# mLSTM heads: squares and denominators folded to 64 partitions each and summed by one product with a two-column selector; memory tokens' squares added over their two parts before they are summed

## The chip, the cores and the metric

One core of one Trainium2 chip. The metric is the device time of one execution in microseconds (us). Matrix products run on TensorE (PE in the profile; its weight loads are PEld), elementwise work on VectorE (DVE), ScalarE (ACT) and GpSimd (POOL); SyncE (SP) issues the DMAs.

## The reference, cut to what matters

One decoder layer, 1024 tokens of width 1024, float32. The part that is changed are the four mLSTM heads (width 128 each) and the norm of 256 memory tokens.

```python
def rmsnorm(x, g):
    xf = x.astype(jnp.float32)
    y = xf * lax.rsqrt(jnp.mean(xf * xf, axis=-1, keepdims=True) + EPS)
    return (y * g.astype(jnp.float32)).astype(x.dtype)
...
        # mlstm_chunkwise, per head, t over tokens
        den = scores.sum(-1) + inter * jnp.einsum('bhd,bhtd->bht', n, qc)
        h = num / jnp.maximum(jnp.abs(den), jnp.exp(-m_t))[..., None]
...
        mh = mlstm_chunkwise(mq, mk, mv, ig, lf)
        mh = mh * lax.rsqrt(jnp.mean(mh * mh, axis=-1, keepdims=True) + EPS)
...
        x = x + cross_attention(rmsnorm(x, ln_x[l]), rmsnorm(mem, ln_mem[l]), w_xq[l], w_xkv[l], w_xo[l])
```

Of each mLSTM head and token two sums over a column are needed: the denominator `den` (over the 128 source rows of the weighted scores) and the sum of the squares of `num` (over the head's 128 columns).

## The kernel before

All large products are split in two parts and made by three products each, `mm3` (L190-194: low by high, high by low, high by high). Every product into float32 has a stationary operand of 128x128 that PEld loads, and up to 512 columns that move past it. The parts themselves come from `split` (L135-142: ACT copies the high part, DVE subtracts it for the low part).

The kernel is written as a sequence of stages, and a scheduler of the framework interleaves them: it sets the order of the instructions of each engine from dependencies and from the program's order, outside stretches that are pinned with `in_order()`. Tiles come from rings of buffers: `w2("c")` is one of two tiles of 128x512 named r_c, `w2("b")` one of two r_b, and the PSUM banks are three sc, two tp, one mm, one m2 (m in the profile) and one ov. An instruction that wants a tile waits until the tile that had the buffer before is read for the last time.

Where the work around the change lies in time (read from the rows of its lines): memory tokens are prepared at about 40 to 100 us (`mem_prepare`, L289-308), and the four heads at about 100 to 395 us. Between and beside the heads' own products PE makes the projections of the next head (`ml_project`), and beside the last head the values of the forgetting attention: `token_major(..., fv_sink)` makes 256-column products into banks tp, mm and m2, and `fv_sink` (L661-664) evacuates each with an ACT copy (L141) and a DVE subtraction (L142) into a tile that rotates over r_b, r_p and r_c. The first scores of the forgetting attention (L754-755) and their masks (L734) come in there too.

In `ml_head` each head is made in two halves of 512 tokens. In a half, for each block of 128 source rows, the scores come from `mm3` into sc, are weighted on DVE (L599), split (L601), and added up over the blocks by GpSimd into `acc` (L603, 128x512, tile r_b); the value products (L605) add up into bank ov. After the last of them the numerator is brought to SBUF (first half: ACT copies it, L613, and squares it, L614; second half: DVE adds the carried part, L609, and ACT squares that, L610), and `sum_cols` (L230-232) makes the column sums on PE: four products with the 128x128 slices of `acc` as weights and one moving column of ones, and four more with the slices of the squares `sq` (tile r_c). ACT takes the absolute denominators (L618) and DVE copies the sums of squares (L619). After the second half follow a chain of small DVE and GpSimd operations that gives the factor of each token, its way through DRAM to a row (`to_row`, L254-261), and the scaling of the numerators (L640-645).

`mem_prepare` adds up the squares of pairs of 128-row slices, so its `acc` of 128x512 has two parts of 256 tokens; `rsqrt_sums` (L243-250) sums both parts with four products of one moving column (two tokens' blocks by two parts).

Of the kernel before, what the change touches and what calls it, by code (L numbers as in the profile page):

```python
# [11 lines left out]
AF = mybir.ActivationFunctionType  # L12
ALU = mybir.AluOpType
# [4 lines left out]
P = 128  # L18
# [4 lines left out]
NM = 256  # L23
# [21 lines left out]
def hybrid_layer(ctx: ExitStack, tc: tile.TileContext, a: dict, out: bass.AP):  # L45
    nc = tc.nc
    v, s, g = nc.vector, nc.scalar, nc.gpsimd
# [11 lines left out]
    def sb(tag, shape, bufs, dt=F32):  # L59
        return pool.tile(shape, dt, tag=tag, name=name(tag), bufs=bufs)  # L60
# [18 lines left out]
    def w2(tag, n=512, dt=F32, p=P):  # L79
        return sb("r_" + tag, [P, 512], BUFS[tag], dt)[:p, :n]  # L80

    def col(tag, n=1, bufs=3):
        return sb("c_" + tag, [P, 8], bufs)[:, :n]
# [3 lines left out]
    def ps_tile(tag):  # L87
        return psum.tile([P, 512], F32, tag=tag, name=name(tag), bufs=PBUFS[tag])

    def sc():  # L90
        return ps_tile("sc")
# [4 lines left out]
    def ov_():  # L96
        return ps_tile("ov")
# [10 lines left out]
    def const(n, shape, dt=F32):  # L108
        return pool.tile(shape, dt, tag=n, name=n, bufs=1)
# [7 lines left out]
    for _ in range(11):  # L117
        nc.tensor.matmul(spun, blank[:, :P], blank, start=True, stop=True)

    ones = const("ones", [P, 1])  # L120
    g.memset(ones, 1.0)
    ident = const("ident", [P, P])
    g.memset(ident, 1.0)
    g.affine_select(out=ident, in_=ident, pattern=[[-1, P]], compare_op=ALU.is_equal, fill=0.0, base=0, channel_multiplier=1)
# [10 lines left out]
    def split(hi, lo, src, scale=None):  # L135

        if scale is None:
            s.activation(hi, src, AF.Copy)  # L138
            return v.tensor_tensor(out=lo, in0=src, in1=hi.bitcast(F32), op=ALU.subtract)  # L139
        else:  # L140
            s.activation(hi, src, AF.Copy, scale=scale)  # L141
            return v.scalar_tensor_tensor(out=lo, in0=src, scalar=scale, in1=hi.bitcast(F32), op0=ALU.mult, op1=ALU.subtract)  # L142
# [53 lines left out]
    def both(pair, f):  # L196
        return f(pair[0]), f(pair[1])
# [32 lines left out]
    def sum_cols(ps, src, n):  # L230
        for t in range(n):
            nc.tensor.matmul(ps[:, t : t + 1], src[:, t * P : (t + 1) * P], ones, start=True, stop=True)

    def square_sum(acc, x, first, by=s, add=v):
        sq = acc if first else w2("c")[:, : x.shape[-1]]
        if by is s:
            s.activation(sq, x, AF.Square)
        else:
            by.tensor_tensor(out=sq, in0=x, in1=x, op=ALU.mult)
        if not first:  # L240
            add.tensor_tensor(out=acc, in0=sq, in1=acc, op=ALU.add)

    def rsqrt_sums(acc, r, nt, parts=1, bank=None, over=None, how=rsqrt_cols):  # L243

        ps = (bank or ov_)()
        for t in range(nt):
            for e in range(parts):
                at = (e * nt + t) * P
                nc.tensor.matmul(ps[:, t : t + 1], acc[:, at : at + P], ones, start=e == 0, stop=e == parts - 1)
        return how(r, ps[:, :nt], 1.0 / D, nt, over)  # L250
# [36 lines left out]
    rcol_m = const("rcol_m", [P, 2])  # L287

    def mem_prepare():  # L289
        acc = w2("b")  # L290
        for i in range(KT // 2):
            if i == 2:
                yield
            raw = w2("f")
            load(raw.rearrange("p (k c) -> p k c", k=2), a["mem"][:, 2 * i : 2 * i + 2])
            hi = w2("p", dt=F32R)
            with tc.issue_after(begun):
                square_sum(acc, raw, i == 0)
                for e in range(2):
                    c = slice(e * NM, e * NM + NM)  # L300
                    gain = vec[:, VEC["ln_mem"] + 2 * i + e :][:, 0:1]
                    split(hi[:, c], raw[:, c].bitcast(F32R), raw[:, c], gain)
            for p_, t in enumerate((hi.bitcast(F32), raw)):
                load(hmd[:, p_, 2 * i : 2 * i + 2], t.rearrange("p (k c) -> p k c", k=2))
        yield
        rsqrt_sums(acc, rcol_m, 2, 2)
        to_row(row_m, rcol_m, 2, rowd[1:2, :NM])
        yield

# [7 lines left out]
    def mv_of(hd, t):  # L317

        return mv[hd // 2][:, t, hd % 2 * 256 : hd % 2 * 256 + 256]
# [15 lines left out]
    for k in range(KT):  # L335
        if k % 2 == 0:
            c = slice(k % 4 * 256, k % 4 * 256 + 512)
# [44 lines left out]
    z, e, q, lf = (small[:, i:j].rearrange("p (t c) -> p t c", c=c) for i, j, c in ((0, 128, GC), (128, 224, GW), (224, 320, GW), (320, 416, GW)))  # L382
# [58 lines left out]
    ps = ov_()  # L441
# [136 lines left out]
    def ml_head(hd, q, k, og, num1, den1):  # L578
        fac = col("fac", 8)
        nums = []  # L580
        dens = col("dens", 8)
        sqs = col("sqs", 8)
        for hf in range(2):
            nmb = w2("a")
            load(nmb, rows[hd : hd + 1, hf * TH : hf * TH + TH].broadcast_to([P, TH]))
            num = ov_()
            acc = den1 if hf else w2("b")
            last = 4 * hf + 3
            for j in range(4 * hf, last + 1):
                d0 = j - 4 * hf  # L590
                c0 = min(d0 * P, 256)
                sp = sc()
                ks = both(k, lambda z: z[:, j * P : (j + 1) * P])
                mm3(sp[:, c0:], ks, both(q, lambda z: z[:, hf * TH + c0 : hf * TH + TH]), True, True)
                wt = acc if j == 0 else w2("c")
                s.activation(wt[:, c0:], nmb[:, c0:], AF.Exp, bias=gcol[:, j, hd : hd + 1])
                n_ = d0 * P + P - c0
                g.affine_select(out=wt[:, c0 : c0 + n_], in_=wt[:, c0 : c0 + n_], pattern=[[1, n_]], compare_op=ALU.is_ge, fill=0.0, base=c0 - d0 * P, channel_multiplier=-1)
                v.scalar_tensor_tensor(out=wt[:, c0:], in0=sp[:, c0:], scalar=float(P) ** -0.5, in1=wt[:, c0:], op0=ALU.mult, op1=ALU.mult)  # L599
                wh, wl = w2("d", dt=F32R), w2("e", dt=F32R)  # L600
                split(wh[:, c0:], wl[:, c0:], wt[:, c0:])  # L601
                if j:
                    g.tensor_tensor(out=acc[:, c0:], in0=wt[:, c0:], in1=acc[:, c0:], op=ALU.add)  # L603
                vj = mv_of(hd, j)
                mm3(num[:, c0:], (vj[:, :P], vj[:, P:]), (wh[:, c0:], wl[:, c0:]), d0 == 0, j == last)  # L605
            sq = w2("c")
            if hf:
                nsb = num1
                v.tensor_tensor(out=nsb, in0=num, in1=nsb, op=ALU.add)  # L609
                s.activation(sq, nsb, AF.Square)  # L610
            else:
                nsb = w2("f")
                s.activation(nsb, num, AF.Copy)  # L613
                s.activation(sq, num, AF.Square)  # L614
            ps = sc()
            sum_cols(ps[:, 0:4], acc, 4)
            sum_cols(ps[:, 4:8], sq, 4)
            s.activation(dens[:, 4 * hf : 4 * hf + 4], ps[:, 0:4], AF.Abs)  # L618
            v.tensor_copy(sqs[:, 4 * hf : 4 * hf + 4], ps[:, 4:8])  # L619
            nums.append(nsb)  # L620
        v.tensor_tensor(out=dens, in0=dens, in1=emc[:, :, hd], op=ALU.max)
        rd = col("rd", 8)
        v.reciprocal(rd, dens)
        v.tensor_tensor(out=sqs, in0=sqs, in1=rd, op=ALU.mult)
        v.tensor_tensor(out=sqs, in0=sqs, in1=rd, op=ALU.mult)
        rsqrt_cols(fac, sqs, 1.0 / P, 8)
        v.tensor_tensor(out=fac, in0=fac, in1=rd, op=ALU.mult)
        yield
        end = hd == MLH - 1
        fbs = [w2("a"), w2("d")] if end else [None, None]  # L630
        at = facd[hd : hd + 1]
        for hf in range(2):
            fb = fbs[hf] or w2("a")
            if hf == 0:
                to_row(fb, fac, 8, at, sc)
            if hf != end:
                load(fbs[1] or fb, at[:, TH:].broadcast_to([P, TH]))
            yield
            y = nums[hf]
            v.scalar_tensor_tensor(out=y, in0=y, scalar=vec[:, VEC["ml_norm"] + hd : VEC["ml_norm"] + hd + 1], in1=fb, op0=ALU.mult, op1=ALU.mult)  # L640
            v.scalar_tensor_tensor(out=y, in0=og[:, hf * TH : hf * TH + TH], scalar=1.0, in1=y, op0=ALU.add, op1=ALU.mult)
            yh, yl = w2("e" if end and hf else "y", dt=F32R), y.bitcast(F32R)
            split(yh, yl, y, 0.5)
            load(mix[hf, 0, :, hd], yh.bitcast(F32))
            load(mix[hf, 1, :, hd], yl.bitcast(F32))
# [59 lines left out]
    for _ in range(2):  # L705
        t = act().rearrange("p a b -> p (a b)").rearrange("p (i c) -> p i c", i=4)
# [403 lines left out]
    for step in fill:  # L1110
        n, e = divmod(halves[0], 2)
# [479 lines left out]
    for at, (b, m) in enumerate(steps):  # L1591
# [14 lines left out]
        x = x2[m // 2][:, m % 2]  # L1606
# [3 lines left out]
        for i, of, y, op in ((1, 1, x22, ALU.add), (5, 5, x22, ALU.add), (7, 7, x22, ALU.add), (6, 6, x22, ALU.add), (2, 1, x11, ALU.add), (4, 5, x21, ALU.subtract), (3, 7, x12, ALU.subtract)):  # L1610
            if of == i:
                held[of] = bank()
            ps = held[of]
# [9 lines left out]
    for i in range(2):  # L1623
        t = act()
# [132 lines left out]
```

## Time and profile before

| what | value |
|---|---|
| median of 3 runs | 1512.55 us (1512.06 to 1512.98) |
| span of the profiled execution | 1510.9 us; the median lies 1.65 us above it |
| PE busy | 1498.5 us (99%) |
| PEld busy | 1259.5 us (83%) |
| DVE busy | 1097.5 us (73%) |
| ACT busy | 717.5 us (47%) |
| POOL busy | 450.6 us (30%) |
| PE's share of the chain that ended last | 98% |

The profiled execution has no run time of its own beside its span; the difference to the median is taken as what lies around the span. Busy times overlap: an engine at 99% with a chain that is made of its own instructions is the one whose work sets the time, and an idle stretch of another engine costs nothing unless PE waits for it. Times in a timeline are from the span's start; a matmul's row shows a start and a duration in which the next one has begun already, so the cost of a product to PE is the distance of the starts, not the duration. Float32 products leave two records each, so `x8` on such a row is four products.

### The profile page before, as it was taken

To read this page: it belongs to the slowest core of one execution; us is meant where nothing else is said; L and a number is where in the kernel's file an instruction comes from. 1 tells how busy PE (TensorE), PEld (TensorE's weight loads), DVE (VectorE), ACT (ScalarE), POOL (GpSimd) and SP (SyncE) were. 2 spreads that over 40 slices of the span, in tenths; PEclk is the share of its full clock that TensorE was granted. 3 is DMA by queue.
4 is the path that set the end of the run, shared out by engine and by line. 5 is a ranking of instruction groups with operands and counts; after the bars stand their busy time and mean duration, and the time that the engine had idled before them with its cause. 6 is when DMAs were issued, how large, how long until landed. Compare 5 with 4: busy or idle time off the path is not lost.

```text
span 1510.9 us, 21868 instructions
## 1 busy us (share of the span) xinstructions
PE 1498.5 (99%) x7708; PEld 1259.5 (83%) x7708; DVE 1097.5 (73%) x1743; ACT 717.5 (47%) x1347; POOL 450.6 (30%) x529
## 2 busy tenths in 40 slices
PE   9999999999999999999999999999999999999997
PEld 8988888889999888888888888888888888888887
DVE  7676676665799875844457988888887788777765
ACT  7343343334788773534444556565656332222134
POOL 0003030413466551001110033344433644343312
PEclk9999999999999999999999999999999999999999
DMA  5332333436889768533334446867766865555623
GB/s 209 117 114 91 115 100 127 129 130 169 279 253 270 218 199 291 198 123 119 119 119 133 154 136 237 281 244 265 272 243 235 352 258 221 223 223 223 251 84 112
DMA packets 114258, 288.33 MB, mean 191 GB/s; under 512 B 12882, under 2 KB 23436, under 8 KB 108516
## 3 DMA queue, kind: packets, MB, share of 16 engines
q1 hardware_dynamic: 113860, 286.83, 56.0%
q8 instruction: 60, 0.98, 0.3%
q14 instruction: 50, 0.41, 0.1%
q10 hardware_dynamic: 288, 0.11, 0.0%
HBM read 194.36 MB, written 92.53 MB: 190 GB/s over the span
## 4 chain that ended last, share of the span: by engine, by line
PE 98%; issue 0%; DVE 0%; DMA 0%; POOL 0%; ACT 0%; POOLq 0%; ACTq 0%; DVEq 0%
PE tp L194 9%; PE tp L193 9%; PE tp L192 9%; PE sc L192 7%; PE sc L194 7%; PE sc L193 7%; PE m L192 6%; PE m L194 6%; PE m L193 6%; PE mm L192 6%; PE mm L193 6%; PE mm L194 6%; PE ov L813 2%; PE ov L192 2%; PE ov L193 2%; PE ov L194 2%
## 5 line engine op out<-in xcount | busy, mean ns | idle before, releaser
L194 PE MATMUL tp<-act,wh 128*128 128x512 f32 (+1 forms) x456 | 178.5, 392 | 0.0
L192 PE MATMUL tp<-act,wl 128*128 128x512 f32 (+1 forms) x456 | 178.5, 392 | 0.0
L193 PE MATMUL tp<-act,wh 128*128 128x512 f32 (+1 forms) x456 | 178.5, 391 | 0.0
L138 ACT ACTIVATE wh<-wr 128x1024 fp32r<-128x1024 f32 (+3 forms) x96 | 92.7, 966 | 95.9 <-PE tp L194 36.6
L139 DVE TENSOR_TENSOR wl<-wr,wh 128x1024 fp32r<-128x1024 f32 (+3 forms) x96 | 113.9, 1187 | 14.5 <-ACT wh L138 14.4
L193 PE MATMUL mm<-act,wh 128*128 128x512 f32 (+1 forms) x320 | 122.6, 383 | 0.0
L192 PE MATMUL mm<-act,wl 128*128 128x512 f32 (+1 forms) x320 | 122.6, 383 | 0.0
L194 PE MATMUL mm<-act,wh 128*128 128x512 f32 (+1 forms) x320 | 122.3, 382 | 0.0
L192 PE MATMUL m<-act,wl 128*128 128x512 f32 (+1 forms) x312 | 119.5, 383 | 0.0
L193 PE MATMUL m<-act,wh 128*128 128x512 f32 (+1 forms) x312 | 118.9, 381 | 0.0
L194 PE MATMUL m<-act,wh 128*128 128x512 f32 (+1 forms) x312 | 118.8, 381 | 0.0
L192 PE MATMUL sc<-act,wl 128*128 128x512 f32 (+1 forms) x268 | 103.8, 387 | 0.0
L193 PE MATMUL sc<-act,wh 128*128 128x512 f32 (+1 forms) x268 | 103.7, 387 | 0.0
L194 PE MATMUL sc<-act,wh 128*128 128x512 f32 (+1 forms) x268 | 103.6, 387 | 0.0
L194 PEld LDWEIGHTS tp<-act,wh 128*128 128x128 f32 x456 | 85.7, 188 | 19.5
L193 PEld LDWEIGHTS tp<-act,wh 128*128 128x128 f32 x456 | 85.8, 188 | 19.0
L192 PEld LDWEIGHTS tp<-act,wl 128*128 128x128 f32 x456 | 85.7, 188 | 19.0
L1491 POOL TENSOR_TENSOR z<-wr 128x256 f32<-128x256 f32 x56 | 50.4, 921 | 147.6 <-DMA wr<-w_ff2q 140.8
L138 ACT ACTIVATE w<-wr 128x768 fp32r<-128x768 f32 (+2 forms) x31 | 25.5, 825 | 133.7 <-PE tp L194 69.2
L138 ACT ACTIVATE wh<-z 128x1024 fp32r<-128x1024 f32 (+2 forms) x55 | 52.5, 956 | 65.0 <-POOL z L1491 28.8
L139 DVE TENSOR_TENSOR wl<-z,wh 128x1024 fp32r<-128x1024 f32 (+2 forms) x55 | 65.9, 1198 | 10.1 <-ACT wh L138 10.1
L194 PEld LDWEIGHTS mm<-act,wh 128*128 128x128 f32 x320 | 60.2, 188 | 12.5
(673 smaller groups left out, 4207.9 us busy)
## 6 DMA issues: line engine op xcount, KB each, us to landing
act<-right SPq DMA_DIRECT2D x35, 1024.0 KB
right<-r_d SPq DMA_DIRECT2D x70, 256.0 KB
right<-w SPq DMA_DIRECT2D x56, 256.0 KB
wr<-w_ff2q SPq DMA_DIRECT2D x28, 512.0 KB
act<-fqk SPq DMA_DIRECT2D x48, 256.0 KB
wr<-w_in SPq DMA_DIRECT2D x20, 512.0 KB
wr<-w_ff SPq DMA_DIRECT2D x20, 512.0 KB
fqk<-r_p SPq DMA_DIRECT2D x32, 256.0 KB
```

The source lines that it names most:

```text
L138: s.activation(hi, src, AF.Copy)
L139: return v.tensor_tensor(out=lo, in0=src, in1=hi.bitcast(F32), op=ALU.subtract)
L192: nc.tensor.matmul(ps, w[1], x[0], start=first, stop=False, skip_group_check=more)
L193: nc.tensor.matmul(ps, w[0], x[1], start=False, stop=False, skip_group_check=more)
L194: nc.tensor.matmul(ps, w[0], x[0], start=False, stop=last, skip_group_check=more)
L813: nc.tensor.matmul(self.ov[:, c0:], self.fv[:, self.j], t[:, c0:], start=self.j == 0 and t is self.p[1], stop=self.last and t is self.p[0])
L1491: g.tensor_tensor(out=o, in0=x, in1=y, op=op)
```

## The change

In the heads, each half's `acc` and `sq` are folded from 128 to 64 partitions by a DVE addition of their lower and upper halves (two additions of 64x512); the folded squares go to partitions 0 to 63 and the folded denominators' parts to partitions 64 to 127 of one tile `folded`, a third tile from the ring of two r_c. Four products follow with the 128x128 slices of `folded` as weights and a moving operand of two columns, `pair_ones`, with ones in one half of the partitions each and zeros in the other, so that each product gives both sums. For memory tokens the two parts of `acc` are added by DVE (128x256), and two products remain of four. Two memsets of 64x1 on GpSimd at the start make the zeros.

```diff
-    ones = const("ones", [P, 1])
-    g.memset(ones, 1.0)
+    units_ = const("ones", [P, 3])
+    ones, pair_ones = units_[:, 0:1], units_[:, 1:3]
+    g.memset(units_, 1.0)
+    for e in range(2):
+        g.memset(pair_ones[64 - 64 * e : 128 - 64 * e, e : e + 1], 0.0)
...
-        rsqrt_sums(acc, rcol_m, 2, 2)
+        v.tensor_tensor(out=acc[:, :NM], in0=acc[:, :NM], in1=acc[:, NM:], op=ALU.add)
+        rsqrt_sums(acc, rcol_m, 2)
...
-            ps = sc()
-            sum_cols(ps[:, 0:4], acc, 4)
-            sum_cols(ps[:, 4:8], sq, 4)
-            s.activation(dens[:, 4 * hf : 4 * hf + 4], ps[:, 0:4], AF.Abs)
-            v.tensor_copy(sqs[:, 4 * hf : 4 * hf + 4], ps[:, 4:8])
+            ps = sc()[:, :8].rearrange("p (t e) -> p t e", e=2)
+            folded = w2("c")
+            for t, x in ((folded[0:64], sq), (folded[64:128], acc)):
+                v.tensor_tensor(out=t, in0=x[0:64], in1=x[64:128], op=ALU.add)
+            for t in range(4):
+                nc.tensor.matmul(ps[:, t], folded[:, t * P : (t + 1) * P], pair_ones, start=True, stop=True)
+            s.activation(dens[:, 4 * hf : 4 * hf + 4], ps[:, :, 1], AF.Abs)
+            v.tensor_copy(sqs[:, 4 * hf : 4 * hf + 4], ps[:, :, 0])
```

Line numbers after the change are higher by 3 from L118 on, by 4 from L310 on and by 7 behind the edit of `ml_head`: L142 before is L145 after, L139 is L142, L609 is L613; the folds are L622, their products L624.

Because the framework orders each engine's instructions anew, the change also moves others, from the memory sums (about 95 us) to the first value products of the forgetting attention (about 390 us); behind that the order of every engine is the same as before. The products that stand between the last value product of a half and the products with its squares are, in the built orders (128x512, 128x256 and 128x128 products; sums that lie between are left out):

| half | before | after |
|---|---|---|
| head 0, first | 24 of 512 | 39 of 512 |
| head 0, second | 19 of 512, 8 of 256, 3 of 128 | 20 of 512, 8 of 256 |
| head 1, first | 24 of 512 | 35 of 512 |
| head 1, second | 30 of 512, 1 of 256 | 26 of 512, 8 of 256 |
| head 2, first | 24 of 512 | 31 of 512 |
| head 2, second | 20 of 512, 8 of 256, 3 of 128 | 20 of 512, 8 of 256 |
| head 3, first | 30 of 256 | 37 of 256 |
| head 3, second | 29 of 256 | 12 of 256 |

The last row of it on PE, before: ov is the numerator of head 3's second half, `L232 ... r_b` are the sums of its denominators, `L232 ... r_c` those of its squares; mm, tp and m are banks of the forgetting attention's values.

```order
L194 MATMUL ov_3087<-r_d_3144,act_107 128x256
L193 MATMUL mm_3504<-wl_3349,act_104 128x256
L194 MATMUL mm_3504<-wh_3348,act_104 128x256
...
L193 MATMUL tp_3533<-wl_3343,act_104 128x256
L232 MATMUL sc_3155<-ones,r_b_2937 128x1 x2
L194 MATMUL tp_3533<-wh_3342,act_104 128x256
...
L194 MATMUL tp_3533<-wh_3348,act_104 128x256
L232 MATMUL sc_3155<-ones,r_c_3152 128x1 x4
L192 MATMUL m_563_3562<-wh_3342,act_105 128x256
```

And after, with the same half's last value product first:

```order
L197 MATMUL ov_3081<-r_d_3138,act_109 128x256
L195 MATMUL tp_3526<-wh_3341,act_107 128x256
L196 MATMUL tp_3526<-wl_3342,act_106 128x256
L197 MATMUL tp_3526<-wh_3341,act_106 128x256
...
L197 MATMUL m_571_3555<-wh_3341,act_106 128x256
L624 MATMUL sc_3149<-ones,r_c_3150 128x2 x4
L761 MATMUL sc_3202<-act_3173 128x256
L762 MATMUL sc_3202<-act_3173 128x256
```

The sums have moved from behind 29 value products to behind 12, and two score tiles with their masks come right behind them.

On DVE at the same place before, from the addition that ends the numerator on; `wl<-wr,wh` of 128x1024 is the split of a weight tile of the values.

```order
L609 TENSOR_TENSOR r_f_2936<-ov_3087,r_f_2936 128x512
L142 SCALAR_TENSOR_TENSOR r_c_3435<-tp_3410,rcol,r_c_3435 128x4x64
L142 SCALAR_TENSOR_TENSOR r_b_3558<-tp_3533,rcol,r_b_3558 128x4x64
L142 SCALAR_TENSOR_TENSOR r_c_3529<-mm_3504,rcol,r_c_3529 128x4x64
L619 COPY c_sqs_3003<-sc_3155 128x4
L621 TENSOR_TENSOR c_dens_3002<-c_dens_3002,emc 128x8
L623 RECIPROCAL c_rd_3167<-c_dens_3002 128x8
L624 TENSOR_TENSOR c_sqs_3003<-c_sqs_3003,c_rd_3167 128x8
L625 TENSOR_TENSOR c_sqs_3003<-c_sqs_3003,c_rd_3167 128x8
L204 TENSOR_SCALAR c_var_3171<-c_sqs_3003 128x8
L139 TENSOR_TENSOR wl_3600<-wr_3597,wh_3599 128x1024
```

And after:

```order
L613 TENSOR_TENSOR r_f_2931<-ov_3081,r_f_2931 128x512
L142 TENSOR_TENSOR wl_3593<-wr_3590,wh_3592 128x1024
L622 TENSOR_TENSOR r_c_3150<-r_b_2932 64x512
L622 TENSOR_TENSOR r_c_3150<-r_c_3146 64x512
L145 SCALAR_TENSOR_TENSOR r_b_3551<-tp_3526,rcol,r_b_3551 128x4x64
L145 SCALAR_TENSOR_TENSOR r_p_3580<-m_571_3555,rcol,r_p_3580 128x4x64
L997 TENSOR_TENSOR wl_3882<-wr_3833,wh_3881 128x512
L145 SCALAR_TENSOR_TENSOR r_c_3428<-tp_3403,rcol,r_c_3428 128x4x64
L626 COPY c_sqs_2998<-sc_3149 128x4
```

The weight tile's split, which stood behind the sums, now stands ahead of the two folds, and the evacuations of the values' banks into r_b and r_c stand behind them.

## The prediction

> **What bounds the kernel now.** I read the page first: the busy times, the granted clock and the chain that ended last.
>
> ```profile
> PE 1498.5 (99%) x7708; PEld 1259.5 (83%) x7708; DVE 1097.5 (73%) x1743; ACT 717.5 (47%) x1347; POOL 450.6 (30%) x529
> PEclk9999999999999999999999999999999999999999
> PE 98%; issue 0%; DVE 0%; DMA 0%; POOL 0%; ACT 0%; POOLq 0%; ACTq 0%; DVEq 0%
> ```
>
> PE is busy throughout, at full clock, and the chain runs through PE alone. Next come PE's waits, all of them, and the stretch of the heads, 100 to 395 us (behind the length: busy us and instructions of PE, PEld, DVE, ACT and POOL, then clock, DMA share, GB/s).
>
> ```profile
> PE ov L228 <- DVE c_r L220: 1.7, 1, 1.7
> PE mm L192 <- DVE act L142: 1.4, 1, 1.4
> PE ov L118 <- DVE r_y L115: 1.2, 1, 1.2
> PE sc L754 <- ACT act L767: 0.7, 1, 0.7
> PE ov L232 <- DVE c_var L1649: 0.5, 1, 0.5
> PE sc L754 <- ACT w L767: 0.4, 1, 0.4
> 100.00:395.00 295.00, 294.27 (x1621) 252.83 (x1620) 190.84 (x325) 115.55 (x216) 69.74 (x88) 1.00 0.43 131
> ```
>
> The waits sum to 5.9 us, and PE's idle time in the heads is 295.00 − 294.27 = 0.73 us, the wait at the first scores. So a product that goes away there gives its whole pitch to the span, and whatever PE newly waits for is lost in full. DVE has 295 − 191 = 104 us free in that stretch.
>
> **The change part by part.** First, the sums that go. The line of the head sums gives their number, and the rows around one group of four the price.
>
> ```profile
> L232 PE MATMUL sc<-ones,r_c x64: 164/250/250, 140.0 to 360.4; 128*128 128x1 f32 x64
> 139.02 0.39 PE L192 MATMUL m<-act,wl 128*128 128x512 f32 x1
> 139.25 0.39 PE L193 MATMUL m<-act,wh 128*128 128x512 f32 x1
> ...
> 139.95 0.95 PE L232 MATMUL sc<-ones,r_c 128*128 128x1 f32 x8
> 140.76 0.36 PE L192 MATMUL sc<-w,w 128*128 128x256 f32 x1
> 140.96 0.28 PE L193 MATMUL sc<-w,w 128*128 128x256 f32 x1
> 141.08 0.28 PE L194 MATMUL sc<-w,w 128*128 128x256 f32 x1
> ```
>
> 64 records, two to a product, are 32 products with the squares, four in each of 8 halves, and as many with the denominators: 64 products before, 32 after. Four took from 139.95 until the 256-column stream was in step again at 140.96; a 256-column product in step takes 141.08 − 140.96 = 0.12 us (one of 512 columns 0.23), so four sums cost 1.01 − 0.12 = 0.89 us, 0.2225 each. 32 fewer are −7.12 us.
>
> The memory tokens' sums are the same kind of product, made where PE is as full; two fewer of four are −0.44 us. The addition that replaces them, 128x256 on DVE, has its inputs many us before the sums; I cost it, like the two memsets at the start, at nothing: what hides it is the value and transpose products that PE makes until then, and uncovered it would cost no more than a fold, below.
>
> The remaining 32 products move two columns instead of one. No row has two columns, but one and 128 are there:
>
> ```profile
> 1478.54 0.95 PE L249 MATMUL ov<-ones,r_b 128*128 128x1 f32 x8
> 1479.35 0.36 PE L192 MATMUL sc<-act,wl 128*128 128x256 f32 x1
> 1479.55 0.28 PE L193 MATMUL sc<-act,wh 128*128 128x256 f32 x1
> ...
> 1482.18 1.05 PE L228 MATMUL ov<-ident,c_r 128*128 128x128 f32 x8
> 1482.98 0.36 PE L192 MATMUL tp<-act,wl 128*128 128x256 f32 x1
> 1483.18 0.28 PE L193 MATMUL tp<-act,wh 128*128 128x256 f32 x1
> ```
>
> Four products of one column take 1479.55 − 1478.54 − 0.12 = 0.89 us, four of 128 columns 1483.18 − 1482.18 − 0.12 = 0.88 us. Nothing changes between one and 128 columns, so two cost the same, and the sum on PE stands at −7.56 us.
>
> Second, the folds. DVE gets 16 additions of 64x512 from SBUF to SBUF, a shape that is there later on, at its least, median and most:
>
> ```profile
> L823 DVE TENSOR_TENSOR r_f<-r_c x16: 686/745/1229, 402.8 to 573.4; 64x512 f32<-64x512 f32 x16
> ```
>
> 16 x 0.745 = 11.9 us against 104 us free: DVE doesn't become the bound. What counts is latency, because the four products now wait for both folds. Here is the half that decides, head 3's second, as it is before:
>
> ```profile
> 355.70 0.28 PE L194 MATMUL ov<-r_d,act 128*128 128x256 f32 x1
> 356.02 0.69 DVE L609 TENSOR_TENSOR r_f<-ov,r_f 128x512 f32<-128x512 f32 x1 [1.28 <-PE ov L194]
> 356.83 0.63 ACT L610 ACTIVATE r_c<-r_f 128x512 f32<-128x512 f32 x1 [1.49 <-DVE r_f L609]
> 359.69 0.95 PE L232 MATMUL sc<-ones,r_c 128*128 128x1 f32 x8
> 360.39 0.48 DVE L142 SCALAR_TENSOR_TENSOR r_b<-tp,rcol,r_b 128x256 fp32r<-128x256 f32 x1 [2.05 <-ACT r_b L141]
> 362.19 1.06 ACT L138 ACTIVATE wh<-wr 128x1024 fp32r<-128x1024 f32 x1 [0.91 <-PE m L194]
> 363.29 1.23 DVE L139 TENSOR_TENSOR wl<-wr,wh 128x1024 fp32r<-128x1024 f32 x1 [0.55 <-ACT wh L138]
> 366.90 0.17 DVE L627 TENSOR_TENSOR c_fac<-c_fac,c_rd 128x8 f32<-128x8 f32 x1
> ```
>
> The squares were ready at 356.83 + 0.63 = 357.46, 1.8 us after the last value product's start, and PE had 4.0 us of other products in front of the sums. Now 12 products of 256 columns stand there, with the last value product itself 13 x 0.12 = 1.5 us. On DVE follow, counted from that product's start: the numerator's addition, +0.32 to +1.01; the weight tile's split, moved ahead of the folds, 1.23 us, to +2.24 (its ACT copy, 1.06 us, is released by a product that stands six places, 0.7 us, ahead of the last value product in the order, and is done by about +0.7; the square follows on ACT, done by +1.8); two folds of 0.745, to +3.73. So PE waits about 3.7 − 1.5 = 2.2 us. Bounds: 1.9 us with folds at 0.686 and the overlap of some 0.1 us that DVE's rows have where they follow each other; 3.2 us with both folds at 1.229; and 0 where PE is late against its order. I take 2.2, the median fold's.
>
> Behind the waiting sums on PE stand two score tiles with masks, whose operands came long ago, and the next value tile, which needs the evacuation of its bank into r_b, the first DVE instruction behind the folds (0.48 us, to +4.2). PE reaches it at 3.7 + 0.89 + about 0.7 = +5.3, so no second wait follows there. The banks evacuated into r_c, whose ring the folded tile has joined, are needed from +8 on and evacuated by about +6 to +7. The factor takes 366.90 + 0.17 − 359.69 = 7.4 us from the sums; some 9 us of products now stand between them and its transpose.
>
> In the other seven halves the order keeps 20 to 39 products of 512 columns (the least: 20 and 8 more of 256), or in head 3's first half 37 of 256: with the value product itself 20 x 0.23 + 9 x 0.12 = 5.7 us or more, and 38 x 0.12 = 4.5 us. The chain there is at most addition, square and two folds, 1.8 + 2 x 0.745 = 3.3 us without other DVE work between. So 2.4 us or more are left, 1.2 in head 3's first half: I cost these at nothing, hidden behind those products. Where one 1.23 us split comes between in head 3's first half the cover is just gone; with slow folds (1.229) as well PE would wait there for 1 us.
>
> The sum: −7.12 − 0.44 + 2.2 = −5.4 us on the span of 1510.9, to 1505.5; the median lies 1.65 us above the span, which gives 1507.2 us. 0.2% (3.0 us) is about what a measurement of this kernel can tell from no change, so the borders are 1509.5 and 1515.6.
>
> **The rivals.** (1) The wait is covered, because PE comes to the half's end later against DVE than its order says. For it: before, PE never waited at these sums. Against it: the order puts 1.5 us of products before a chain of 3.7. −7.56 us: 1505.0, and 1503.9 if the score waits of 0.7 and 0.4 us go as well.
>
> (2) The wait takes the clock down. One wait of 0.73 us left it at 1.00; in the tail it fell:
>
> ```profile
> 392.00:394.00 2.00, 1.27 (x9) 1.05 (x8) 1.65 (x5) 1.92 (x8) 0.00 (x0) 1.00 1.09 326
> ...
> 1503.00:1503.50 0.50, 0.00 (x0) 0.00 (x1) 0.32 (x2) 0.00 (x0) 0.00 (x0) 1.00 0.00 0
> 1503.50:1504.00 0.50, 0.47 (x2) 0.50 (x3) 0.00 (x0) 0.00 (x0) 0.00 (x0) 0.61 0.00 0
> 1503.53 1.11 PE L228 MATMUL ov<-ident,c_r 128*128 128x128 f32 x4 [1.72 <-DVE c_r L220]
> ```
>
> It fell at about 1503.6, after waits of 0.5 and 1.72 us close together: 2.2 us, as much as I forecast, though there PE had little work between. No row shows how long a lowered clock stays under full work. If it stays as long as it took to fall from the last full stretch (about 1500 to 1503.6), 3.6 us at half speed lose 1.8 us: 1507.2 + 1.8 = 1509.0, and 1510.0 with the wait at its upper bound. (The Trainium skill, "TensorE: Matmul & The Clock Gate", Part 1, says that the clock falls to half after a whole idle window of about 3.4 us and comes back after as long a busy one, and warns of gaps above some 3 us: by it a wait of 2.2 us costs nothing more, and one above 3.4 us some 1.7 us. The tail's row, with PE idle 1.72 us at a stretch when it fell, is nearer to the rival than that rule.)
>
> (3) The other side: the folds come late in every half, because DVE has splits queued ahead of them and runs two-input additions slowly beside GpSimd's. For it: the folds' own row reaches 1.229 us. Against it: DVE is free a third of the stretch, and PE waited for no DVE result in these 295 us. With 3.2 us in head 3's second half and w in each of the other seven the time is 1505.0 + 3.2 + 7w; it is slower from w = (1515.6 − 1508.2) / 7 = 1.06 us on. With a split and two slow folds, 3.3 + 1.23 + 0.97 = 5.5 us against 5.7, w is still about zero; it takes a second split, w = 1.0 to 1.3, 1515 to 1517.3.
>
> (4) The reordering brings one or two further waits: head 3's first half (1 us, above), the scores at 392 us (0.7 and 0.4 before) or a bank whose evacuation stands behind the folds, 1 to 3 us more than the forecast: 1508.3 to 1510.3.
>
> (5) The change doesn't do what it says: two moving columns cost as two sums. Then the heads save nothing on PE, −0.44 + 2.2, 1514.3. The 128-column rows speak against it.
>
> **How the numbers follow.** Chances: forecast 0.49 (1506.2 to 1508.3, the wait's bounds and a few tenths), (1) 0.19, (2) 0.10, (3) 0.05, (4) 0.14, (5) 0.03. Below 1509.5 lie the forecast, (1), three quarters of (2) and two thirds of (4): faster 0.49 + 0.19 + 0.075 + 0.09 = 0.84, which I lower to 0.82, since the order holds what I call hidden to within 1.2 us at one place. Slower is most of (3), 0.04; the rest, 0.14, is the same. The range from 1504.0 to 1510.4 leaves out the best of (1) and what lies above (2) and (4), about 1 in 8; it is left no wider, since the price of the sums is fixed to 0.1 us.
>
> **What would show it.** In the profile after: four products 128x2 with 0.89 us from their start until the next stream is in step; 32 of them in the heads and two one-column products of the memory tokens; the folds at about 0.75 us; one new row among PE's waits, at the sums of head 3's second half on the second fold, of 1.9 to 3.2 us; clock 1.00 in the stretch after it; and everything from the first value products of the forgetting attention on shifted by about 5.4 us. I am wrong if that wait is missing (1), if the clock falls behind it (2), if the same wait stands in many halves (3), or if PE waits at other lines between 100 and 400 us (4).

## The result, and the profile after

The changed kernel takes 1516.32 us (median of 10 runs, 1512.56 to 1520.22) against 1512.51 us (10 runs, 1511.90 to 1514.23): a ratio of 1.0023, 95% interval 1.0015 to 1.0032, slower. 1507.2 us had been forecast. The profiled execution took 1515.79 us with a span of 1514.1 us, 3.2 us above that of before. Its page, and the stretch of the heads:

```profile
PE 1494.4 (99%) x7640; PEld 1251.8 (83%) x7640; DVE 1106.5 (73%) x1760; ACT 717.1 (47%) x1347; POOL 451.8 (30%) x531
PE 96%; DVE 2%; DMA 1%; issue 1%; ACT 0%; POOL 0%; POOLq 0%; DVEq 0%; ACTq 0%; SPq 0%
100.00:395.00 295.00, 287.59 (x1539) 244.42 (x1537) 199.22 (x334) 113.18 (x207) 70.90 (x87) 0.99 0.42 129
```

PE has 68 records fewer, which are the 34 products, but it now stands idle for 295.00 − 287.59 = 7.4 us of the heads' stretch, where it stood idle for 0.7. The chain goes through DVE and DMA in places, and the mean clock of the stretch is 0.99. The rows at which PE waits there and shortly behind, from the timeline:

```profile
156.40 0.28 PE L197 MATMUL ov<-r_d,act 128*128 128x256 f32 x1
158.05 0.39 PE L555 MATMUL tp<-act,r_e 128*128 128x256 f32 x1 [1.38 <-DVE r_e L142]
158.28 0.28 PE L555 MATMUL tp<-act,r_d 128*128 128x256 f32 x1
...
294.08 0.39 PE L195 MATMUL ov<-r_d,act 128*128 128x256 f32 x1 [0.68 <-ACT r_d L141]
295.47 0.39 PE L196 MATMUL ov<-r_e,act 128*128 128x256 f32 x1 [1.01 <-DVE r_e L142]
...
297.71 0.39 PE L555 MATMUL tp<-act,r_e 128*128 128x256 f32 x1 [1.38 <-DVE r_e L142]
...
363.42 1.05 PE L624 MATMUL sc<-ones,r_c 128*128 128x2 f32 x8 [2.02 <-DVE r_c L622]
...
382.48 0.50 PE L761 MATMUL sc<-act 128*128 128x512 f32 x1 [0.69 <-ACT act L774]
395.61 0.44 PE L761 MATMUL sc<-act 128*128 128x384 f32 x1 [0.72 <-ACT act L774]
```

The last one was there before (0.73). The wait at 363.42 us is the one forecast, at head 3's sums. The other five are new: L555 are the products that carry a head's state from its first half of tokens to its second (L551 before), here of heads 1 and 3, made of keys that DVE has just split (r_e); the rows at 294 and 295 us are value products of head 2's second half, and the one at 382 us is a score of the forgetting attention. Each costs some 0.26 us more than the bracket says: from 156.40 to 158.28 are 1.88 us where 0.24 would be the pitch of two products, 1.64 us lost for a wait of 1.38, and the same reckoning gives 0.26 us a wait at the other five.

The wait at 158 us can be followed back on ACT and DVE, and that at 382 us too:

```profile
156.35 0.60 ACT L141 ACTIVATE r_d<-mm 128x512 fp32r<-128x512 f32 x1 [1.10 <-PE ov L197]
156.71 0.69 DVE L613 TENSOR_TENSOR r_f<-ov,r_f 128x512 f32<-128x512 f32 x1
157.32 0.68 DVE L142 TENSOR_TENSOR r_e<-mm,r_d 128x512 fp32r<-128x512 f32 x1
158.03 0.69 DVE L622 TENSOR_TENSOR r_c<-r_b 64x512 f32<-64x512 f32 x1
...
380.89 0.75 DVE L647 SCALAR_TENSOR_TENSOR r_f<-r_f,vec,r_a 128x512 f32<-128x512 f32 x1 [2.85 <-DMA r_a<-facd]
381.86 0.47 ACT L774 ACTIVATE act<-sc,c_mx 128x256 f32<-128x256 f32 x1 [4.11 <-DVE c_den L782]
```

The high part of the keys goes into a tile of the ring r_d, which also holds the weights of the value products. ACT had to wait 1.10 us for a value product before it could copy the keys, DVE subtracted the low part behind the numerator's addition, and the fold (L622) came only after that: no fold lies in this wait. At 381 us DVE had stood 2.85 us for the transfer that brings head 3's factors as a row; the small DVE operations ahead of a softmax exponential (L774) stood behind it, and PE waited for that exponential.

Behind the three waits close together the clock fell:

```profile
297.00:298.00 1.00, 0.29 (x2) 0.29 (x3) 0.97 (x3) 0.63 (x1) 0.00 (x0) 1.00 0.00 0
298.00:299.00 1.00, 1.00 (x7) 1.00 (x7) 0.90 (x2) 0.00 (x0) 0.00 (x0) 0.54 0.00 0
299.00:300.00 1.00, 1.00 (x5) 0.90 (x5) 0.30 (x2) 0.28 (x1) 0.00 (x0) 0.50 0.00 0
300.00:301.00 1.00, 1.00 (x3) 0.73 (x3) 0.45 (x2) 0.31 (x1) 0.00 (x0) 0.50 0.00 0
301.00:302.00 1.00, 1.00 (x5) 0.79 (x4) 0.00 (x0) 0.00 (x0) 0.00 (x0) 0.76 0.07 25
```

The column behind POOL's is the clock: at half for 0.92 + 1 + 1 + 0.48 = 3.4 us, in which PE is full, so 1.7 us are lost. The account of the span: −7.6 us of products, +7.2 us of waits by their brackets (1.38 + 0.68 + 1.01 + 1.38 + 2.02 + 0.69), +1.6 us at six restarts, +1.7 us of clock: +2.9 of the measured +3.2 us. The last 0.3 us isn't found in single rows.

### The profile page after: what moved, and what is told of

It reads as the page before. It is cut to its first block, busy times and chain, and to the rows that moved or that the text cites. A ratio compares the mean times of both kernels' runs of the same rounds, so it can differ in the third digit from the quotient of the medians.

```text
span 1514.1 us, 21755 instructions
## 1 busy us (share of the span) xinstructions
PE 1494.4 (99%) x7640; PEld 1251.8 (83%) x7640; DVE 1106.5 (73%) x1760; ACT 717.1 (47%) x1347; POOL 451.8 (30%) x531
## 4 chain that ended last, share of the span: by engine, by line
PE 96%; DVE 2%; DMA 1%; issue 1%; ACT 0%; POOL 0%; POOLq 0%; DVEq 0%; ACTq 0%; SPq 0%
PE tp L195 8%; PE tp L196 8%; PE tp L197 8%; PE sc L195 6%; PE sc L196 6%; PE sc L197 6%; PE m L195 6%; PE m L197 6%; PE m L196 6%; PE mm L195 6%; PE mm L197 6%; PE mm L196 6%; PE ov L820 2%; PE ov L196 2%; PE ov L195 2%; PE ov L197 2%
## 5 line engine op out<-in xcount | busy, mean ns | idle before, releaser
L142 DVE TENSOR_TENSOR wl<-wr,wh 128x1024 fp32r<-128x1024 f32 (+3 forms) x96 | 113.7, 1186 | 17.0 <-ACT wh L141 16.7
L142 DVE TENSOR_TENSOR wl<-z,wh 128x1024 fp32r<-128x1024 f32 (+2 forms) x55 | 65.9, 1199 | 11.0 <-ACT wh L141 10.8
```

## The experiments

Four theories stand against each other. A: what costs is the new order. The PSUM bank of a half's sums and the tiles of the r_c ring are handed out in program order; before, the denominators' sums took the bank early, and the next half's scores could follow. Now its first writer waits for both folds, and the scores stand behind it, so that a second half's work comes bunched. B: what costs is the folds' time and latency on DVE. C: a large part is the clock that falls behind waits. D: the third tile in the ring of two is what holds things up. That the scores have moved is seen in the rows of head 0, the first scores of its second half, before and then after:

```profile
127.77 0.28 PE L232 MATMUL sc<-ones,r_b 128*128 128x1 f32 x2
127.91 0.48 PE L192 MATMUL sc<-w,w 128*128 128x512 f32 x1
```

```profile
144.09 0.95 PE L624 MATMUL sc<-ones,r_c 128*128 128x2 f32 x8
144.90 0.48 PE L195 MATMUL sc<-w,w 128*128 128x512 f32 x1
145.21 0.39 PE L196 MATMUL sc<-w,w 128*128 128x512 f32 x1
```

In both they come right behind the first product into the sums' bank, which is 16 us later now. (The second fence also gives the price of the four products, 145.21 − 144.09 − 0.23 = 0.89 us, as forecast.)

**The order alone, by two lines.** In the kernel before, the two calls that make the sums are swapped; nothing is folded.

```diff
-            sum_cols(ps[:, 0:4], acc, 4)
             sum_cols(ps[:, 4:8], sq, 4)
+            sum_cols(ps[:, 0:4], acc, 4)
```

> The kernel before, with nothing folded: all 64 products of one column stay, only the two calls that make the sums of a half are swapped, squares first. Theory A (the bank): the PSUM tile of the sums is handed out in program order; before, the denominators' sums take it early and the next half's scores can follow; once its first writer waits for the squares, the next scores stand behind the sums on PE, and the second half's value products and the next head's state products come bunched, closer than ACT and DVE can follow. Then this kernel shows most of the new waits of the kernel after without any fold: at the state products of heads 1 and 3 about 1.4 us each, at the value products of a second half 1 to 2 us, none at the sums; 4 to 5 us of waits, 1516 to 1519 us with a fall of the clock (1.7 us) in some runs. Theory B (the folds): the waits come from the folds' time on DVE and their latency; then 1512.5 us as before, within 1 us, and no new row among PE's waits.

1515.41 us, ratio 1.0021 (1.0012 to 1.0031). Three waits, at places where after has them:

```profile
159.48 0.38 PE L551 MATMUL tp<-act,r_e 128*128 128x256 f32 x1 [1.39 <-DVE r_e L139]
...
298.46 0.39 PE L192 MATMUL ov<-r_d,act 128*128 128x256 f32 x1 [0.16 <-ACT r_d L138]
299.72 0.39 PE L551 MATMUL tp<-act,r_e 128*128 128x256 f32 x1 [0.30 <-DVE r_e L139]
```

Theory A by its kind, at 1.9 us of waits instead of 4 to 5, and faster than the 1516 to 1519 us expected. With all products kept and no fold in it, this kernel is slower by 2.4 us (1512.99 us for before beside it). The changed kernel is slower by 3.8 us although it saves 7.6, so it loses 11.4 us in all: the two lines account for about a fifth of that.

**The order alone, all of it.** The kernel before, with a table that fixes the order of every engine between 95 and 400 us to that of after (each listed instruction is made to follow the one ahead of it on its engine; the eight sums of a half stand where the four stand).

```diff
+    for nums in json.loads(zlib.decompress(base64.b85decode("".join(PINNED)))).values():
+        for p_, n_ in zip(nums, nums[1:]):
+            tc.add_manual_dep(by[f"I-{n_}"], f"I-{p_}", ...)
```

> The kernel before, all sums of one column and nothing folded, with the order of every engine between 95 and 400 us fixed to that of the kernel after; the eight sums of a half stand where after's four stand. Theory A, strong form (the order alone makes all new waits but that on the folds): waits of 5 us at state products, value products and scores, 1517 to 1519 us. Theory A with B (the order makes the place tight, the folds' time on DVE does the rest): about 2 us of waits as with the two calls swapped, 1514.5 to 1515.5 us. Theory B alone: 1512.5 us.

1528.97 us, ratio 1.0103 (1.0085 to 1.0121): 13 us above the changed kernel itself, of which 7.6 us are the sums that it still makes. Among its waits are the same ones as after's again, 1.38 us at the state products of heads 1 and 3 (160.79 and 308.75 us) and 0.68 us on r_d (304.54 us), and it has longer ones besides. The strong form of A expected too little. An order can thus cost this much without any fold, but only part of these waits are after's, so the run doesn't measure how much of after's own loss the order is. The clock was at 0.993 over its span.

**Another bank.** The sums of after go to the numerators' bank.

```diff
-            ps = sc()[:, :8].rearrange("p (t e) -> p t e", e=2)
+            ps = ov_()[:, :8].rearrange("p (t e) -> p t e", e=2)
```

> The kernel after, with the sums' products written to the numerators' bank ov in place of one of the three score banks; the folds stay as they are. Theory A: the next half's scores are free of the sums again; the waits at value products of second halves (1.7 us with head 2) and at head 3's sums (2.0 us) go. The state products still stand directly behind the last value product in heads 1 to 3, so up to three waits of 1.4 us stay: 1505 + 4.2 = 1509 us (1506 to 1511). Theory B: the same folds at the same places on DVE, so 1515 to 1517 us as after.

1532.11 us, ratio 1.0129 (1.0113 to 1.0144). The expectation was 23 us off: the scores are free, but the next half's value products now share the bank with the sums, the framework laid out yet another order, and its longest waits are at places that no theory named (6.8 us on DVE's w, L690; 3.6 us at three value products). The run changes the bank and the order at once, so it can't tell the two apart.

**The bank claimed early**, with eight zeroed columns ahead of the square:

```diff
+            bank = sc()[:, :8]
+            v.memset(bank, 0.0)
+            ps = bank.rearrange("p (t e) -> p t e", e=2)
             sq = w2("c")
```

> The kernel after with one thing more: the sums' score bank is taken, and 8 of its columns set to zero by DVE (128x8, eight times), ahead of the half's square in the program, so that the bank is handed out early as before and later scores needn't stand behind the sums. Scores of second halves stand ahead of the sums on PE again; the state products still come right behind the last value product of heads 1 to 3. Theory A (the sums' bank, taken late, bunches the work): the waits at second halves' value products (1.7 us) go and the one at head 3's sums shrinks to 0.6 us, up to three of 1.4 us at state products stay: 1506 to 1511 us. Theory B (folds on DVE): 1515 to 1518 us as after.

1521.46 us, ratio 1.0054 (1.0038 to 1.0070), above what either theory expected. The wait at head 3's sums is gone, the scores of second halves stand early, but a wait of 5.3 us at 269.19 us (on DVE's r_f, L575) has come and the waits at head 2 and 3 have stayed. Freeing the bank is no cure as long as the framework chooses the order.

**The order of before, with the change in it.** PE's order is fixed by a table as above, to that of before; first with the sums in bank ov and folded in place (`folded = sq`):

> The whole change, the sums in bank ov, folded in place (the squares' tile takes both folds, no third tile of its ring), and PE's order between 95 and 400 us fixed to that of the kernel before, with the four products of a half about 2.9 us of work behind the half's square, where the eight were or a little ahead. Theory A: the order was what cost; the products that went are gained in full, 1512.5 - 7.6 = 1505 us (1504 to 1507), clock 0.998, no new PE wait over 0.5 us. Theory B: the 16 folds on DVE make PE wait at several halves, 1508 us or more. Theory C (what costs is the clock falling behind waits): also 1505 us, since there are no waits.

1509.51 us, ratio 0.9977 (0.9967 to 0.9986): the sign turns. The waits of after are gone; 1.36 us at the ov bank, 0.85 us at a transpose and 0.33 us at the sums are new. Theory A had expected 1504 to 1507 us and no new wait over 0.5 us; the time lies where theory B had put it, though of the new waits only the 0.33 us is for a fold. With the score bank claimed early, once with the third tile and once in place:

> The claim kernel with PE's order of 95 to 400 us fixed to that of the kernel before, the four products of a half about 2.9 us of work behind its square. Beside the order and the early bank it is the kernel after: the folds go to a third tile of the ring of two. Theory A: as with the order fixed and bank ov, but without the wait of 1.4 us for that bank: 1506 to 1508 us, clock 0.998. Theory B: waits on the folds (DVE r_c at the sums) in several halves, 1509 us or more. Theory D (the third tile in the ring of two is what holds things up): waits at value products on DVE r_e, 1 to 2 us more than with folding in place.

1509.86 us, ratio 0.9976 (0.9967 to 0.9986). It is above the 1506 to 1508 us that theory A expected. But against the kernel with the bank claimed early (1521.46 us, run beside it) it differs in nothing but PE's order, folds and third tile included, and that is worth 11.6 us, by waits and by the clock behind them (mean 0.993 and 0.998 in the two traces). Of all the runs this pair tests theory A most directly.

> The same with the folds in place (the squares' tile takes both), so without a third tile. Theory A: within 1 us of the one with the third tile, 1506 to 1508 us. Theory D: 1 to 2 us faster than that one.

1508.08 us, ratio 0.9966 (0.9952 to 0.9979). The medians stand 1.8 us apart as theory D has it, though the intervals overlap. The trace with the third tile shows four waits of 0.3 to 1.4 us, that without two (1.14 us at a transpose, 0.34 us at the sums). Only one of the four, of 0.29 us, is at a value product, where theory D had expected them; two are at the sums (0.47 and 0.53 us). So D is neither shown nor excluded. Last, DVE's order of before as well, and the sums exactly where they were:

> The whole change, folds in place, the score bank claimed early, PE's order of the kernel before with the four products exactly where the eight were, and DVE's order of before as well up to about 345 us, the two folds behind the square in places where DVE waited before. Theory A (order): the two waits that were left (1.1 us at a transpose on DVE's r_b, 0.3 us at the sums) go, 1508.1 - 1.8 = 1506.3 us, 1505 to 1507; -7.6 us of sums as in the prediction's first term, and 0 to 1 us lost. Theory B (the folds' time on DVE costs by itself): waits on DVE results of 0.5 us or more remain at several halves, 1508 us or more.

1505.64 us (1505.23 to 1506.10), ratio 0.9952 (0.9940 to 0.9965), the fastest of all. Its waits of PE, all of them, and the heads' stretch:

```profile
PE ov L231 <- DVE c_r L223: 1.7, 1, 1.7
PE ov L118 <- DVE r_y L115: 1.2, 1, 1.2
PE sc L763 <- ACT act L776: 0.9, 2, 0.7
PE ov L235 <- DVE c_var L1658: 0.5, 1, 0.5
PE sc L763 <- ACT w L776: 0.4, 1, 0.4
PE m L195 <- DVE wl L142: 0.2, 1, 0.2
100.00:390.00 290.00, 288.75 (x1567) 247.09 (x1566) 202.54 (x354) 116.87 (x220) 73.08 (x93) 1.00 0.44 135
```

No wait of the heads is left, and DVE is as busy as in after. Against the runs of before beside it (1513.10 us) 7.5 us are gained, where the products alone come to 7.56. This version also has the early bank and the folds in place; that most of the step is the order's is shown by the pair above.

**Are the folds covered?** The same kernel, with the denominators' fold issued three times.

```diff
-            for t, x in ((folded[0:64], sq), (folded[64:128], acc)):
+            for t, x in ((folded[0:64], sq), (folded[64:128], acc), (folded[64:128], acc), (folded[64:128], acc)):
```

> The fastest version so far (1505.6 us: order of before on PE and DVE, bank claimed, folds in place) with the denominators' fold issued three times in place of once: 16 more additions of 64x512 on DVE, 0.69 us each, in front of the sums and of what follows on DVE. It measures the cover of the folds. By the prediction's count 5.7 us of products stand behind the last value product of most halves and the chain takes 3.3 us, so 2.4 us are left and 1.4 us more of folds change nothing there; DVE itself waited 1.0 to 2.6 us at these places: 1505 to 1507 us. Theory B (folds on DVE cost PE time by themselves): 0.7 to 1.4 us lost in each of 8 halves, 1511 us or more.

1523.05 us, ratio 1.0061 (1.0047 to 1.0075), 17 us for 16 additions, where 1505 to 1507 us had been expected.

```profile
PE sc L626 <- DVE r_c L624: 7.3, 4, 2.4
PE tp L549 <- DVE r_b L546: 1.4, 1, 1.4
```

```profile
134.62 0.69 DVE L624 TENSOR_TENSOR r_c<-r_b 64x512 f32<-64x512 f32 x1
138.10 0.95 PE L626 MATMUL sc<-ones,r_c 128*128 128x2 f32 x8
...
351.27 0.69 DVE L624 TENSOR_TENSOR r_c<-r_b 64x512 f32<-64x512 f32 x1
352.11 1.03 PE L626 MATMUL sc<-ones,r_c 128*128 128x2 f32 x8
```

The first fence is of this kernel. The second is of the one without the extra folds, with the second fold and the sums of head 0's first half and of head 3's second half. At four of eight sums PE now waits, 7.3 us in all, and the clock falls behind each of them. In the fastest version the second fold ends 2.8 us ahead of the sums in the first halves of heads 0 to 2 (138.10 − 134.62 − 0.69), 1.9 us ahead in head 1's second half, and 0.15 to 0.75 us ahead in the other four halves, which are the four that now wait. In after the folds end 2.35 to 5.8 us ahead of the sums in the seven halves that the prediction called hidden. So the order that gains most leaves the folds less cover than after's, and at four places less than the 1.4 us of two more folds. Theory B is right so far: the folds cost nothing only as long as nothing is added at these places.

**The parts apart.** The memory tokens' part alone, and the heads' alone:

> The memory tokens' part alone (two products fewer, one addition of 128x256 on DVE); heads as before. PE's order moves at 153 products between 95 and 230 us, with all scores ahead of the sums as before and the state products some products behind the last value product, so no new waits: -0.4 us, 1512.0 to 1513.0 us, too little to be told from the kernel before. If any edit that makes the framework order anew brings waits, 1514 us or more.

1513.47 us, ratio 1.0003 (0.9995 to 1.0012): no difference, and the 0.44 us of its two products is too little to be seen in it.

> The heads' part alone. Its order has the scores of second halves behind the sums and the state products of heads 1 and 3 right behind the last value products, as after: -7.1 us of sums, 5 us of waits there and 1.5 to 2.5 us at head 3's sums, a fall of the clock or two: 1514 to 1519 us, with the waits at the same places as after. If the memory part had been needed for it, 1505 to 1508 us.

1517.74 us, ratio 1.0025 (1.0014 to 1.0036), with the waits of after at the same places (1.38 us at 159.10 and 298.02, 1.01 us at 295.78, 2.13 us at the sums at 363.85 us). Its trace is of the slowest run, 1523.53 us, and has further waits behind the heads. The loss belongs to the heads' part.

**The changed kernel once more**, for a second trace:

> The kernel after, once more, for another trace of it. Theory C: the waits are the same each time, and the time changes with how often the clock falls to half for one stretch behind them; each fall costs about 1.7 us. The times spread from 1512.5 to 1520 us as before, and the trace shows the same waits (7 to 8 us in 100 to 395 us) and none to four stretches of clock 0.5, the time following their number. If the waits themselves change from run to run, the sum of the waits differs by the spread instead.

1517.82 us, ratio 1.0026 (1.0016 to 1.0036). The waits at 158, 295, 297 and 363 us are the same to 0.01 us, and those of 0.7 us at 294 and 382 us are missing, yet the span is 1.9 us longer. The clock fell behind two waits at head 2's end, and here they are, in this trace:

```profile
294.65 0.39 PE L196 MATMUL ov<-r_e,act 128*128 128x256 f32 x1 [1.01 <-DVE r_e L142]
296.90 0.39 PE L555 MATMUL tp<-act,r_e 128*128 128x256 f32 x1 [1.38 <-DVE r_e L142]
297.00:298.00 1.00, 1.00 (x8) 1.00 (x9) 0.90 (x2) 0.00 (x0) 0.00 (x0) 0.82 0.00 0
298.00:299.00 1.00, 1.00 (x4) 0.84 (x4) 0.60 (x2) 0.28 (x1) 0.00 (x0) 0.50 0.00 0
```

Next are the windows around head 3's sums, in the first trace and in this one:

```profile
362.00:363.00 1.00, 0.00 (x0) 0.00 (x0) 0.90 (x2) 1.00 (x3) 0.20 (x1) 1.00 0.77 167
363.00:369.00 6.00, 5.58 (x47) 5.49 (x48) 4.10 (x16) 2.27 (x8) 4.00 (x3) 1.00 0.89 261
```

```profile
362.00:363.00 1.00, 0.38 (x2) 0.38 (x3) 1.00 (x3) 0.83 (x2) 1.00 (x1) 0.75 0.96 172
363.00:369.00 6.00, 6.00 (x28) 5.81 (x29) 3.43 (x13) 1.64 (x7) 3.19 (x3) 0.50 0.96 296
```

The same wait of 2.02 us took the clock down in one execution, for some 6.8 us, and not in the other. That is 3.4 us lost, more than the whole difference of the two spans. It bears out theory C as far as the spread goes: of the first ten runs the fastest, 1512.56 us, had a mean clock of 0.998 (as before has), the slowest, 1520.22 us, one of 0.994. It isn't the whole: at 0.997 stand both 1514.01 and 1517.99 us.

## Why the prediction was wrong, point by point

- The sums that go: right. 0.89 us for four, with two columns as with one; the fastest version gains 7.5 of the 7.56 us.
- The memory tokens' addition: right. It takes 0.43 us at 48.4 us, 47 us ahead of its sums, and the part alone moves nothing.
- Head 3's second half: right. 2.02 us against 2.2 (the folds took 0.69 us each, not 0.745).
- "In the other seven halves ... I cost these at nothing, hidden behind those products": here it failed. At the sums of those halves there is indeed no wait. But I had counted the products ahead of the sums alone, and not looked at what the new order puts behind them. The next half's scores had moved behind the sums, the state products directly behind the last value product (1.65 us in after, 159.27 − 154.85 = 4.4 us before), and none of these places was read. The five new waits are 5.1 us by their brackets, 6.4 with the restarts, and the clock behind three of them adds 1.7: 8.1 of the 8.6 us by which the span missed the forecast (1514.1 against 1505.5 us). Rival (4) had this kind of thing, with one or two waits of 1 to 3 us and a chance of 0.14; its places were others.
- The factor of head 3: costed at nothing, with some 9 us of products ahead of its transpose. PE didn't wait there, but DVE stood 2.85 us for the factors' row, and that ended as the wait of 0.69 us at a score (382 us).
- The folded tile's place in the r_c ring was followed only to the evacuations of values beside head 3. In after, ACT's exponentials for the next half's weights waited 8.6 us in four waits for the folds. Whether any of PE's waits comes from that isn't shown.
- Rival (2), the clock: its price was right for the fall at head 2's end (1.8 us, 1.7 measured), though by luck in part, since no row stood for how long a lowered clock stays; behind the forecast wait itself, where the second trace has a fall, 3.4 us were lost. The chance of 0.10 was far too small, because it was tied to one wait of 2.2 us: three waits that sum to 3.1 us brought the clock down in the first trace, and two that sum to 2.4 us within 3.3 us in the second. The Trainium skill ("TensorE: Matmul & The Clock Gate", Part 1) has the clock come back after about 3.4 us of work, and the trace agrees at head 2's end, with 3.4 us at half in both traces; behind head 3's sums it was 6.8 us. It asks for a whole idle window of that length for the fall; here PE had work in between, 2.6 of the 5 us from 293 to 298 us in the second trace, and 2.02 us of idleness sufficed once, so the measurement decides against reading it as one gap of 3.4 us.
- The chances: 0.82 for faster rested on terms for which rows stood. The order was no such term, though its excerpts were at hand: it isn't enough to cost an edit where it stands if the edit also moves many other instructions.

What stays open: 0.3 us of the span; which of the two rings, bank or r_c, moves the order more; why the clock fell behind one wait of 2.02 us and not behind the other; and why the framework's own order with the bank claimed early is the worse one.

## What to carry to other kernels

Where tiles are handed out in program order, the moment of a tile's first write is part of the schedule: an edit that makes a small result wait for more inputs also holds back everything that takes the same ring behind it. On a kernel whose bound engine is full, read the new order at every place where that engine takes a fresh result, not only at the edited lines, and if the order decides, fix it: the same change was worth +0.2% with the order it was given and −0.5% with the old one, there with the bank claimed early and the folds in place. Several short waits close together can cost more than their sum: here the clock fell behind 2.4 us of waits within 3.3 us.

## What the runs showed of the hardware that was not expected

- A wait of PE cost about 0.26 us more than its bracket (1.64 against 1.38 us at 158 us): the first two products behind it start late, by 0.15 and 0.11 us.
- Two waits of 2.02 us at the same place, one with the clock at 1.00 behind it and one with it at half for some 6.8 us.
- An addition of 64x512 in SBUF took 0.69 us in all 16 places of the heads, into the lower and the upper partitions alike. A subtraction of 128x512 in SBUF took 0.67 us (L142, at 153.11 us), so half the partitions saved nothing.
